# Statistics tiles of nine entries a row instead of five: what moves behind them in SBUF

## The chip, the core and the metric

The kernel runs on one core of a Trainium2 chip. The metric is the device time of one execution in microseconds. A run gives several executions; the median is quoted with the lowest and the highest. A profile is one execution recorded instruction by instruction. TensorE (PE) multiplies, VectorE (DVE) and ScalarE (ACT) do elementwise work, GpSimd (POOL) and SyncE (SP) mostly issue transfers. SBUF is the memory beside the engines: 128 partitions, in each of which a tile takes the same range of bytes.

## The reference

One layer of an encoder on 256 tokens of width 2048, in float32. With `mod = silu(c) @ mod_w + mod_b` cut into six rows of 2048:

```python
hmix = x * (1.0 + sc_m) + sh_m
y = windowed_gqa_sink(hmix, ...)      # q, k, v projection, rotary positions, attention with a sink, output projection
x = layer_norm(alpha * x + (1.0 + g_m) * y, ln_mix_g, ln_mix_b)
hff = x * (1.0 + sc_f) + sh_f
y = square(relu(hff @ w1 + b1)) @ w2 + b2
x = layer_norm(alpha * x + (1.0 + g_f) * y, ln_mlp_g, ln_mlp_b)
```

`layer_norm` takes the mean and the variance of each token's 2048 numbers. The weights are some 290 MB, read once.

## The kernel before, in words

**Numbers.** Every float32 operand is split into a high part that TensorE multiplies in its rounded float32 format (`fp32r`) and a low part that is the rest; a product is three matmuls (high x high, high x low, low x high; `mm3`, lines 556 to 558; in the feed-forward part also lines 1161 to 1163, and 1189 with 1191, where two of the three share one matmul of 512 columns).

**Stages.** The first stage (to about 160 us) computes the modulation vectors and the q, k, v projection; then come attention and its output projection (to about 360 us), the first layer norm, and the feed-forward part in four blocks of 2048 hidden units, the last three of which mix the two weight matrices (`ff_mixed`). The second layer norm and the stores end it.

**The stream of weights.** `Stream` loads the weights in an order written out by hand, 1 MB at a time, into tiles `raw` (line 229, SyncE's queue): 8 KB in each of 128 partitions. Five such buffers last the whole kernel and three more the first stages. From each, ScalarE makes the high part (`wh`, line 299) and VectorE the low part (`wl`, line 250). A raw buffer is loaded again when its readers are done. The modulation weights are either multiplied on TensorE straight from raw (`quad`, line 363) or summed on VectorE (line 403). What shifts the modulated input is `modulated` (lines 579 to 581); line 666 is a filler matmul on a constant tile `onesr`.

**Order.** A scheduler places the instructions by priorities (`first(name)` with the table `AHEAD`), and where `keep_in_program_order` is used, as written. Neither looks at the size of a tile.

**Statistics.** For each token the mean and the variance come from `bn_stats`, six numbers for a piece of a row, and `bn_aggr`, which joins the pieces of a row to mean and variance. The tile `st0` is for tokens 0 to 127, `st1` for 128 to 255. Tokens 0 to 127 have four pieces of 512; tokens 128 to 255 have three of 512 and two of 256, five entries. Both tiles are made twice, for the two layer norms, with two buffers each. The aggregations are at line 864 (in `deviation`) and line 1389.

**Where tiles lie.** Pools are laid out one behind the other in SBUF, each tile rounded up to 32 bytes: constants (`cst`), small tiles (`sml`), then `raws`, `whp`, `wlp`, `gen` and the pool that is first `raws2` and later `gen2`. Inside `sml` the order is that of first use: `sc`, `mrow`, the softmax columns, `warm`, then `st0` and `st1`, then the four temporaries of tag `t2` (rl, uf, sf, tmp, gb, w and others, 2048 bytes each), then the columns of the layer norms. In the kernel before:

| tile | first byte in a partition | over a multiple of 512 |
|---|---|---|
| onesr | 18016 | 96 |
| sc, mrow | 20480, 24576 | 0, 0 |
| st0 (two buffers), st1 (two buffers) | 29312, 29440, 29568, 29696 | 128, 256, 384, 0 |
| temporaries of tag t2 | 29824 and each 2048 on | 128 |
| raw (five buffers) | 38784 and each 8192 on | 384 |
| wh, wl, g, and the late raw and g4b | 79744 and each 4096 on | 384 |

Of the kernel before, what the change touches and what calls it, by code (L numbers as in the profile page):

```python
# [11 lines left out]
F32 = mybir.dt.float32  # L12
# [9 lines left out]
NT = S // 128  # L22
# [39 lines left out]
def hybrid_kernel(ctx: ExitStack, tc: tile.TileContext, a, out: bass.AP):  # L62
    nc = tc.nc
    cst = ctx.enter_context(tc.tile_pool(name="cst", bufs=1))
    sml = ctx.enter_context(tc.tile_pool(name="sml", bufs=4))
# [21 lines left out]
    def g4(dt=F32):  # L87
        return gen.tile([128, 1024], dt, tag="g4", name="g4")
# [102 lines left out]
    def first(name):  # L191
        n = AHEAD.get((stage[0], name), AHEAD.get(name))
        return tc.high_priority(n) if n else nullcontext()
# [358 lines left out]
    def part(tiles, t, c):  # L552
        return tiles[c][:, t * 512:t * 512 + 512]

    def mm3(ps, xh, xl, wh, wl, start, stop):
        nc.tensor.matmul(ps, xh, wh, start=start, stop=False)  # L556
        nc.tensor.matmul(ps, xh, wl, start=False, stop=False)  # L557
        S.prev = nc.tensor.matmul(ps, xl, wh, start=False, stop=stop).ins  # L558
# [277 lines left out]
    def add_gated(ps, t, c, gt, stats, n=1, h=0, counted=True):  # L836
        tmp = sml.tile([128, 512], F32, name="tmp", tag="t2", bufs=4)
        cols = slice(h * 512 // n, (h + 1) * 512 // n)
        z = part(xs, t, c)[:, cols]
        with first("gated"):  # L840
            nc.vector.tensor_tensor(tmp[:, cols], ps[:, cols], gt(c)[:, cols], op=OP.mult)
            nc.vector.tensor_add(z, z, tmp[:, cols])
            if counted:
                nc.vector.bn_stats(stats[t][:, c + h], z)

    def by_halves(ps, factors, gated):

        for h in range(2):
            cols = slice(h * 256, h * 256 + 256)
            for n, (xh, xl, wh, wl) in enumerate(factors):  # L850
                mm3(ps[h][:, cols], xh, xl, wh[:, cols], wl[:, cols], n == 0, n == len(factors) - 1)
            gated(h)

    sc = []
    tight = [False]

    def kept(i):
        return tc.keep_in_program_order(i) if tight[0] else i

    def deviation(st=None, mv=None, between=lambda: None):  # L860
        with first("deviation"):
            if mv is None:
                mv = sml.tile([128, 2], F32, name="mv")
                kept(nc.vector.bn_aggr(mv, st))
            sd = sml.tile([128, 1], F32, name="sd")
            kept(nc.scalar.activation(sd, mv[:, 1:2], AF.Sqrt, bias=eps))
            ve = sml.tile([128, 1], F32, name="ve")
            kept(nc.vector.tensor_scalar_add(ve, mv[:, 1:2], LN_EPS))
            between()
            r0 = sml.tile([128, 1], F32, name="r0")  # L870
            kept(nc.vector.reciprocal(r0, sd))
            q = sml.tile([128, 1], F32, name="qq")
            kept(nc.vector.scalar_tensor_tensor(q, r0, ve, r0, op0=OP.mult, op1=OP.mult))
            kept(nc.vector.scalar_tensor_tensor(q, q, -3.0, r0, op0=OP.add, op1=OP.mult))
        return mv, q

    def normed(c, t):
        mv, rstd = sc[t]
        z = part(xs, t, c)
        with first("normed" if c else "normed0"):  # L880
            if t and c == 1:
                nm = sml.tile([128, 1], F32, name="nmr")
                kept(nc.vector.scalar_tensor_tensor(nm, mv[:, 0:1], -1.0, rstd, op0=OP.mult, op1=OP.mult))
                sc.append(nm)
            if t and c:
                kept(nc.scalar.activation(z, z, AF.Identity, scale=rstd, bias=sc[2]))
            else:
                kept(nc.vector.tensor_scalar(z, z, mv[:, 0:1], rstd, op0=OP.subtract, op1=OP.mult))
# [23 lines left out]
    def project(j, c):  # L912
        wh, wl = S.main()
        oh, ol = oT[j]
        pss = [psa.tile([128, 512], F32, name="pa") for _ in range(NT)]
        last = j == 3 and c == 3
        def of(t, r):
            s = slice(t * 512 + r * 128, t * 512 + r * 128 + 128)
            return oh[:, s], ol[:, s], wh(r), wl(r)

        for t, rs in [(0, range(4))] if last else [(t, (r, r + 1)) for r in (0, 2) for t in range(NT)]:
            for r in rs:
                mm3(pss[t], *of(t, r), r == 0, r == 3)
            if t == 1:
                S.done()
            if t == 1 and rs[0] == 0:
                yield
        if last:
            S.done(False)
            add_gated(pss[0], 0, c, g1, st)  # L930
            sc.append(deviation(st[0][:, :4]))
            normed(0, 0)
            yield
            two = [pss[1], psa.tile([128, 512], F32, name="pa")]
            by_halves(two, [of(1, r) for r in range(4)], lambda h: add_gated(two[h], 1, c, g1, st, 2, h))
            S.done(False)
            turn_over()
            tight[0] = True
            sc.append(deviation(st[1]))
            normed(0, 1)  # L940
            S.nl = NLOW
        with first("project"):
            for t, ps in enumerate(pss):
                if j == 0:
                    nc.vector.tensor_add(part(ys, t, c), ps, bo(c))
                elif j < 3:
                    y = part(ys, t, c)
                    nc.vector.tensor_add(y, y, ps)
                    if j == 2:
                        z = part(xs, t, c)  # L950
                        nc.vector.tensor_mul(y, y, g1(c))
                        nc.vector.scalar_tensor_tensor(z, z, ALPHA, y, op0=OP.mult, op1=OP.add)
                elif not last:
                    add_gated(ps, t, c, g1, st)
# [22 lines left out]
    for n in range(21):  # L977
        j, i = n // 4, n % 4
        if n < 16:
            scores(n)  # L980
        for f in todo:
            f()
        todo = []
        if n == 1:
            S.deep = False
        if n == 5:
            assert all(h is raws for h in S.home[S.at:]), "an early buffer is still in use"
        if n + 1 < len(LATE):
            w = qkv(*LATE[n + 1])
        else:  # L990
            if n == 5:
                ys, bo = [g4b() for _ in range(4)], bias_all(a["bo"], [g4b(), g4b()])
            w = project((n - 5) // 4, (n - 5) % 4)
        mid = mids(n)
        if j < 3:
            if i == 0:
                turn = rope(j + 1, 1)
            if 0 < i < 3 or n and i == 0:
                mid.append(lambda: qA.__setitem__(j + 1, next(turn)))
            if i == 3:  # L1000
                mid.append(lambda: qT.__setitem__(j + 1, pairs_T(qA[j + 1], 4)))
        run(w, mid)
        if n == 0:
            next(turn)
        if 0 < n <= 16 and n % 2 == 0:
            todo.append(values(n - 1))
        if n == 9:

            for c in range(4):
                xs[c] = g4()  # L1010
                i = nc.gpsimd.dma_start(xs[c].rearrange("p (t n) -> p t n", t=NT), a["x"][:, :, 512 * c:512 * c + 512])
                tc.add_manual_dep(i.ins, S.prev.name, AFTER, reason="not sooner")
        if n == 12:
            g1 = gate(m_gm)
        if n == 16:
            warm = sml.tile([128, 1], F32, name="warm")
            nc.scalar.activation(warm, eps, AF.Sqrt)
            st = [sml.tile([128, 5, 6], F32, name=f"st{t}", bufs=2) for t in range(NT)]


    def ff_input(g):
# [299 lines left out]
    for n in range(2):  # L1321
        for h in range(2):
            nc.gpsimd.dma_start(gb[n][h], a["lnrow"][2 + n:3 + n, h * 1024:h * 1024 + 1024].partition_broadcast(128))
    st = [sml.tile([128, 5, 6], F32, name=f"st{t}", bufs=2) for t in range(NT)]
    mid = gather(pm)
    for f in mid[:2]:
        f()
# [26 lines left out]
    mv, rstd = deviation(st[0][:, :4])  # L1354
# [31 lines left out]
    keep = tc.keep_in_program_order  # L1386
    with tc.high_priority(200):
        mv = sml.tile([128, 2], F32, name="mv")
        keep(nc.vector.bn_aggr(mv, st[1]))
        dm = sml.tile([128, 128], F32, name="dm", tag="t2", bufs=4)  # L1390
        keep(nc.vector.tensor_scalar(dm, ident, mv[:, 0:1], 0.5, op0=OP.mult, op1=OP.mult))
        rstd = deviation(mv=mv, between=lambda: keep(nc.vector.scalar_tensor_tensor(
            part(xs, 1, 3), part(xs, 1, 3), mv[:, 0:1], gneg, op0=OP.subtract, op1=OP.mult)))[1]
# [99 lines left out]
```

## Time and profile before

| | |
|---|---|
| median of 3 runs | 1071.91 us (1071.26 to 1072.69) |
| profiled execution | 1070.93 us |
| its span, first to last instruction | 1069.1 us |
| TensorE busy | 1056.9 us (99%) |
| VectorE busy | 941.8 us (88%) |
| ScalarE busy | 619.7 us (58%) |
| mean granted TensorE clock | 0.998 |
| bytes moved by the DMA engines | 292.72 MB, 274 GB/s over the span |

A group in the profile is read as: line, engine, operation, output tile <- input tiles, shapes, count | busy us, mean ns of one | idle time of the engine before them, and what ended it. PE's matmuls overlap, so the mean duration of one is longer than the distance from one to the next. The prediction shows the lines that it uses.

### The profile page before, as it was taken

What the parts mean: (1) busy time and instruction counts of PE and PEld (TensorE: products, weight loads), DVE (VectorE), ACT (ScalarE), POOL (GpSimd) and SP (SyncE); (2) the same over time, 40 slices, a digit from 0 to 9 for tenths busy, and PEclk for the clock granted to TensorE, in tenths of its full rate; (3) what the DMA queues carried; (4) which work ended last, traced back from release to release, by engine and by line L of the source; (5) the groups of instructions that cost most, each with busy time, mean ns of one, the idle gap of its engine ahead of it and who ended that gap; (6) DMA issues with size and microseconds to landing.
All of it is one profiled execution on the core that took longest, in us unless ns stands there. A gap on an engine that the chain in (4) does not pass through costs nothing.

```text
span 1069.1 us, 16015 instructions
## 1 busy us (share of the span) xinstructions
PE 1056.9 (99%) x6181; PEld 858.2 (80%) x6181; DVE 941.8 (88%) x1407; ACT 619.7 (58%) x976; POOL 27.4 (3%) x54
## 2 busy tenths in 40 slices
PE   9999999999999999999999999999999999999998
PEld 7677677666677899988888888888888888888886
DVE  4689999989999898987579899889889987999998
ACT  5433347776772647643367776447677446777740
POOL 1000000001000000000000000000000001000000
PEclk9999999999999999999999999999999999999999
DMA  9999998799965897788624644974564783465642
GB/s 378 419 420 420 418 421 323 274 382 355 385 258 198 335 384 296 273 327 346 243 95 182 236 176 179 354 275 161 193 234 157 292 322 132 163 236 197 256 178 78
DMA packets 43516, 292.72 MB, mean 274 GB/s; under 512 B 5152, under 2 KB 5280, under 8 KB 9648
## 3 DMA queue, kind: packets, MB, share of 16 engines
q1 hardware_dynamic: 39456, 279.85, 67.5%
q0 software_dynamic: 3232, 10.50, 2.9%
q10 hardware_dynamic: 752, 1.35, 0.4%
q8 instruction: 48, 0.79, 0.3%
q14 instruction: 28, 0.23, 0.1%
HBM read 289.57 MB, written 2.11 MB: 273 GB/s over the span
## 4 chain that ended last, share of the span: by engine, by line
PE 91%; DVE 4%; DMA 2%; ACT 2%; issue 1%; DVEq 0%; ACTq 0%
PE pa L556 16%; PE pa L558 15%; PE pa L557 15%; PE pa L1189 15%; PE pa L1191 8%; PE pm L363 4%; PE pa L1163 3%; PE pa L1162 3%; PE pa L1161 3%; PE pa L769 2%; PE pa L830 1%; PE pt L813 1%; PE pa L666 1%; DVE wl L250 1%; DMA raw<-in_w2s 1%; PE pt L557 1%
## 5 line engine op out<-in xcount | busy, mean ns | idle before, releaser
L299 ACT CAST wh<-raw 128x1024 fp32r<-128x1024 f32 (+1 forms) x332 | 336.1, 1020 | 264.8 <-PE pa L558 138.5
L250 DVE TENSOR_TENSOR wl<-raw,wh 128x1024 fp32r<-128x1024 f32 (+1 forms) x332 | 388.5, 1181 | 70.6 <-ACT wh L299 64.4
L556 PE MATMUL pa<-wh,g 128*128 128x512 f32 (+1 forms) x652 | 259.7, 399 | 3.9 <-ACT g L579 3.9
L557 PE MATMUL pa<-wl,g 128*128 128x512 f32 (+1 forms) x652 | 254.7, 391 | 0.0
L558 PE MATMUL pa<-wh,g 128*128 128x512 f32 (+1 forms) x652 | 254.0, 391 | 0.2 <-DVE g L581 0.2
L1189 PE MATMUL pa<-g,wh 128*128 128x512 f32 x768 | 192.4, 392 | 0.1
L1189 PEld LDWEIGHTS pa<-g,wh 128*128 128x128 f32 x768 | 140.5, 188 | 29.6 <-issue 0.8
L556 PEld LDWEIGHTS pa<-wh,g 128*128 128x128 f32 x652 | 122.6, 188 | 41.5 <-issue 6.2
L558 PEld LDWEIGHTS pa<-wh,g 128*128 128x128 f32 x652 | 122.8, 188 | 28.3 <-issue 1.6
L557 PEld LDWEIGHTS pa<-wl,g 128*128 128x128 f32 x652 | 122.9, 188 | 24.6 <-DVE scm L444 0.4
L1191 PEld LDWEIGHTS pa<-g,wl 128*128 128x128 f32 x768 | 104.7, 190 | 7.6
L1191 PE MATMUL pa<-g,wl 128*128 128x256 f32 x768 | 107.0, 282 | 0.0
L403 DVE SCALAR_TENSOR_TENSOR g<-raw,cact,g 128x1024 f32<-128x1024 f32 (+1 forms) x69 | 86.2, 1256 | 1.2 <-DMA raw<-in_modf 0.7
L1161 PE MATMUL pa<-g,wh 128*128 128x256 f32 x240 | 67.9, 285 | 0.4 <-ACT wh L299 0.4
L1163 PE MATMUL pa<-g,wh 128*128 128x256 f32 x240 | 67.6, 285 | 0.0
L1162 PE MATMUL pa<-g,wl 128*128 128x256 f32 x240 | 67.5, 284 | 0.0
L250 DVE TENSOR_TENSOR raw<-raw 128x1024 fp32r<-128x1024 f32 x48 | 58.4, 1221 | 0.7 <-ACT raw L299 0.6
L299 ACT CAST raw<-raw 128x1024 fp32r<-128x1024 f32 x48 | 49.8, 1043 | 5.6 <-DVE raw L261 4.5
L403 DVE SCALAR_TENSOR_TENSOR g4b<-raw,cact,g4b 128x1024 f32<-128x1024 f32 x32 | 40.5, 1277 | 6.9 <-DMA raw<-in_modgf 6.9
L1161 PEld LDWEIGHTS pa<-g,wh 128*128 128x128 f32 x240 | 45.9, 192 | 0.8 <-ACT wh L299 0.8
L1162 PEld LDWEIGHTS pa<-g,wl 128*128 128x128 f32 x240 | 45.8, 192 | 0.7 <-issue 0.4
L599 DVE TENSOR_TENSOR g<-g,pa 128x512 f32<-128x512 f32 x60 | 39.6, 682 | 7.5 <-PE pa L558 7.0
(235 smaller groups left out, 1282.0 us busy)
## 6 DMA issues: line engine op xcount, KB each, us to landing
raw<-in_w1b SPq DMA_DIRECT2D x48, 1024.0 KB, 6.6
raw<-in_w SPq DMA_DIRECT2D x40, 1024.0 KB, 7.3
raw<-in_modm SPq DMA_DIRECT2D x32, 1024.0 KB, 12.0
raw<-in_modf SPq DMA_DIRECT2D x32, 1024.0 KB, 7.0
raw<-in_wqkv SPq DMA_DIRECT2D x24, 1024.0 KB, 14.0
raw<-in_w2s SPq DMA_DIRECT2D x24, 1024.0 KB, 4.9
raw<-in_modgm SPq DMA_DIRECT2D x16, 1024.0 KB, 7.7
raw<-in_wo SPq DMA_DIRECT2D x16, 1024.0 KB, 6.8
```

Of the source, the lines that this page charges most:

```text
L250: self.pinned(nc.vector.tensor_sub(l[:, :w], r, f32(self.hs[n])[:, :w]))
L299: self.pinned(nc.scalar.copy(h[:, :s.shape[-1]], s))
L363: i = nc.tensor.matmul(self.ps[32 * j:32 * j + 32, :w], lhsT[j] if type(lhsT) is list else lhsT, rhs[j], start=self.first, stop=stop)
L403: nc.vector.scalar_tensor_tensor(p[:, :e], s, cact[:, kt:kt + 1], p[:, :e], op0=OP.mult, op1=OP.add)
L556: nc.tensor.matmul(ps, xh, wh, start=start, stop=False)
L557: nc.tensor.matmul(ps, xh, wl, start=False, stop=False)
L558: S.prev = nc.tensor.matmul(ps, xl, wh, start=False, stop=stop).ins
L1161: nc.tensor.matmul(o, wh(w, 128), hh, start=new, stop=False)
L1162: nc.tensor.matmul(o, wl(w, 128), hh, start=False, stop=False)
L1163: nc.tensor.matmul(o, wh(w, 128), hl, start=False, stop=end)
L1189: nc.tensor.matmul(ps, wh(k, 128), ff_in(k), start=k == 0, stop=False)
L1191: nc.tensor.matmul(ps[:, :256], wl(k, 128), ff_in(k)[:, :256], start=False, stop=k == NK - 1)
```

## The change

The statistics tiles have nine entries a row instead of five. What is written to them stays; the two aggregations that read a whole row of `st1` now name its first five entries.

```diff
-            sc.append(deviation(st[1]))
+            sc.append(deviation(st[1][:, :5]))
...
-            st = [sml.tile([128, 5, 6], F32, name=f"st{t}", bufs=2) for t in range(NT)]
+            st = [sml.tile([128, 9, 6], F32, name=f"st{t}", bufs=2) for t in range(NT)]
...
-    st = [sml.tile([128, 5, 6], F32, name=f"st{t}", bufs=2) for t in range(NT)]
+    st = [sml.tile([128, 9, 6], F32, name=f"st{t}", bufs=2) for t in range(NT)]
...
-        keep(nc.vector.bn_aggr(mv, st[1]))
+        keep(nc.vector.bn_aggr(mv, st[1][:, :5]))
```

A buffer of a statistics tile grows from 120 to 216 bytes in a partition, with the rounding from 128 to 224. All tiles behind the four buffers begin 384 bytes later: the large tiles 256 bytes over multiples of 512, the temporaries at multiples of 512.

## The prediction

> **What bounds the kernel now.** I began with the page: busy times, the slices with the granted clock and the transfer rate, and the chain of work that ended last.
>
> ```profile
> span 1069.1 us, 16015 instructions
> PE 1056.9 (99%) x6181; PEld 858.2 (80%) x6181; DVE 941.8 (88%) x1407; ACT 619.7 (58%) x976; POOL 27.4 (3%) x54
> PEclk9999999999999999999999999999999999999999
> DMA  9999998799965897788624644974564783465642
> GB/s 378 419 420 420 418 421 323 274 382 355 385 258 198 335 384 296 273 327 346 243 95 182 236 176 179 354 275 161 193 234 157 292 322 132 163 236 197 256 178 78
> PE 91%; DVE 4%; DMA 2%; ACT 2%; issue 1%; DVEq 0%; ACTq 0%
> ```
>
> TensorE is busy for all but 12.2 us, and nine tenths of the chain is TensorE. The transfers fill the first six slices (about 160 us) at a plateau near 420 GB/s and are loose afterwards. Then I asked for the busy times by stretch.
>
> ```profile
> core 0: us, PE busy (x) PEld busy (x) DVE busy (x) ACT busy (x) POOL busy (x), PEclk, DMA share, GB/s
> 0.00:27.00 27.00, 25.43 (x206) 19.21 (x206) 12.44 (x29) 13.87 (x20) 4.96 (x16) 1.00 0.94 379
> 27.00:160.00 133.00, 127.90 (x970) 93.58 (x967) 115.71 (x168) 50.63 (x67) 1.85 (x2) 0.99 1.01 419
> 160.00:400.00 240.00, 239.27 (x1526) 179.80 (x1525) 225.68 (x425) 153.11 (x340) 9.02 (x14) 1.00 0.83 321
> 400.00:1069.00 669.00, 664.29 (x3488) 565.60 (x3486) 587.97 (x787) 402.05 (x549) 11.62 (x22) 1.00 0.60 224
> ```
>
> TensorE's idle time is 1.6 us at the start, 5.1 us in the saturated stretch, 0.7 us up to 400 us and 4.7 us after that. Whatever the change does to the queues, ScalarE or VectorE can pay only inside these small sums; what it does to each matmul would be paid in full. Two pauses and one slow spell make most of the 5.1 us; I read them in the timelines of TensorE and ScalarE and in the chain (start, us, what; in brackets the idle time before it and its releaser).
>
> ```profile
> 45.51 1.04 ACT L299 CAST wh<-raw 128x1024 fp32r<-128x1024 f32 x1 [2.08 <-PE pa L558]
> 47.11 0.50 PE L556 MATMUL pa<-wh,g 128*128 128x512 f32 x1 [1.64 <-ACT g L579]
> ...
> 114.78 1.99 ACT L299 CAST wh<-raw 128x1024 fp32r<-128x1024 f32 x2 [4.74 <-DMA raw<-in_wqkv]
> 117.33 0.50 PE L556 MATMUL pa<-wh,g 128*128 128x512 f32 x1 [1.23 <-ACT g L579]
> ```
>
> ```profile
> 45.02 0.23 PE pa L557
> ...
> 48.89 0.43 PE pa L557
> ...
> 51.45 0.43 PE pa L557
> ```
>
> The pause before 47.1 us is a loop through TensorE itself: the modulation (L579) stands on ScalarE behind a cast (L299) that waited for a matmul to give back its buffer. After it, matmuls follow each other at 0.43 us instead of 0.23 us until 51.9 us, some seven of them and part of an eighth: about 1.5 us. Only the pause before 117.3 us hangs on a transfer (1.23 us).
>
> **The change part by part.** First, the aggregations. They read the first five entries of each row, the same 30 numbers as before, so no instruction, wait or DMA is added or removed, and no queue is passed.
>
> ```profile
> L864 DVE BATCH_NORM_AGGREGATE mv<-st x3: 254/265/285, 349.4 to 1051.8; 128x2 f32<-128x24 f32 x2, 128x2 f32<-128x30 f32 x1
> L1389 DVE BATCH_NORM_AGGREGATE mv<-st x1: 291/291/291, 1060.9 to 1060.9; 128x2 f32<-128x30 f32 x1
> ```
>
> Two instructions of 30 elements are concerned (one of L864, and L1389). Both lie on the path: the square root on ScalarE waits for them. Six elements more, 24 to 30, cost at most 291 - 254 = 37 ns, so even a form that read a few more would be worth under 0.08 us for both. I take 0.
>
> Second, the addresses. Four statistics buffers (two names, two buffers each) grow from 120 to 216 bytes, that is from 128 to 224 in steps of 32, so everything allocated behind them moves up by 4 x 96 = 384 bytes. Measured against multiples of 512, the large tiles (raw, wh, wl, g, g4b) go from 384 to 256 and the temporaries of tag t2 (rl, uf, sf, tmp, gb, w) from 128 to 0. The tiles ahead of them stay: sc and mrow at 0, onesr at 96. Moved tiles keep their distances from each other, since all shift alike; new are the place against fixed boundaries and the distance to what stayed. The trace has no operation on a tile at 256, so each price comes from the nearest rows: operations of one shape on tiles at 0, 96, 128 and 384.
>
> VectorE and ScalarE (groups by shape, mean ns behind the bar):
>
> ```profile
> L264 DVE TENSOR_TENSOR raw<-raw 128x512 f32<-128x512 f32 x24 | 16.4, 684 | 0.0
> L1123 DVE TENSOR_TENSOR sc<-sf,sc 128x512 fp32r<-128x512 f32 x24 | 16.4, 684 | 0.0
> L581 DVE TENSOR_TENSOR g<-g,g 128x256 fp32r<-128x256 f32 x16 | 6.8, 423 | 0.4
> L1109 DVE TENSOR_TENSOR g<-uf,g 128x256 fp32r<-128x256 f32 x48 | 20.2, 421 | 3.3 <-ACT g L1108 3.3
> L299 ACT CAST wh<-raw 128x512 fp32r<-128x512 f32 x24 | 14.9, 620 | 9.5 <-PE pa L1189 5.8 <-DMA raw<-in_w2s 3.5
> L1122 ACT CAST sc<-sf 128x512 fp32r<-128x512 f32 x24 | 14.8, 617 | 6.1 <-DVE sf L1121 6.1
> ```
>
> With every operand at 384 a subtraction of 512 takes 684 ns; with operands at 128 and 0, also 684. At 256 elements, 423 with all at 384 against 421 with one at 128. The casts take 620 (384 to 384) and 617 (128 to 0). Where two operands share a place, as after the change sf and sc will, the raw-raw row says that sharing is free. I take 0. The bounds are 3 ns an instruction: 1407 + 976 instructions make 7 us of engine time, and at the 4% and 2% of the chain that these engines hold, 3 x 1407 x 0.04 + 3 x 976 x 0.02 is about 0.2 us either way.
>
> TensorE, in the same view and in the timeline (merged runs of one instruction):
>
> ```profile
> L556 PE MATMUL pa<-wh,g 128*128 128x512 f32 x644 | 257.4, 401 | 3.9 <-ACT g L579 3.9
> L1189 PE MATMUL pa<-g,wh 128*128 128x512 f32 x768 | 192.4, 392 | 0.1
> L558 PE MATMUL pa<-wh,sc 128*128 128x512 f32 x24 | 9.8, 408 | 0.0
> L557 PE MATMUL pt<-raw,sc 128*128 128x512 f32 x24 | 9.4, 392 | 0.0
> L557 PE MATMUL pt<-wl,g 128*128 128x512 f32 x24 | 9.5, 396 | 0.0
> L557 PE MATMUL pa<-raw,g 128*128 128x512 f32 x24 | 9.3, 388 | 0.0
> ...
> 12.09 4.59 PE L666 MATMUL pa<-onesr 128*128 128x512 f32 x19
> ...
> 570.50 2.00 PE L1189 MATMUL pa<-g,wh 128*128 128x512 f32 x8
> ```
>
> Nineteen matmuls on onesr, at 96, start (4.59 - 0.40) / 18 = 0.233 us apart; eight on g and wh, at 384, (2.00 - 0.40) / 7 = 0.229 us, the 0.40 being the last one's own duration. A place that is a multiple of 32 only thus costs at most 4 ns more than one that is a multiple of 128. The other comparison is inside the mixed stage of the feed-forward part: its twelve groups of 24 that take their weights from sc (at 0) run from 392 to 408 ns, mean 396; the six groups of 24 that take them from g run from 388 to 396, mean 393. That is 3.4 ns, and it doesn't look like the address: the spread within each set is several times larger, and one tile gives both 392 and 408. I take 0. If the 3.4 ns belong to a distance of 128 between weights and moving rows, they change only for these 288 matmuls: 1.0 us, either way. If they belong to multiples of 256 as such, they would come to every matmul; that is a rival below.
>
> Transfers into raw. All destinations of large loads lie at 384 or 128, so no row shows one at 256 or 0. The nearest rows are the full slices, 418 to 421 GB/s over changing mixtures of loads: 0.7% of 160 us, 1.1 us, is what a slower destination may cost by them. A gain of any size reaches the end only through the 1.23 us before 117.3 us, since the larger pause is fed by TensorE. Bounds: -1.2 to +1.1 us. I take 0, the middle: the plateau looks like one rate that the loads share.
>
> [...]
>
> The sum: 0 + 0 + 0 + 0 on the profiled execution's 1070.9 us (span 1069.1, and 1.8 us around it), which is 1.0 us under the median of the runs. So I forecast the median again: **1071.9 us**.
>
> **The rivals.** (1) The loads get shorter. The wait before 117.3 us closes, 1.2 us: 1070.7 us. If the earlier arrivals also take away the pause that comes before the slow spell, its 1.5 us go as well: 1071.9 - 2.7 = 1069.2 us. For it: the share of 1.01 over 133 us. Against it: TensorE's larger pause is fed by TensorE, and behind 160 us the queues have slack (0.83, 0.60), so an earlier load only waits longer.
>
> (2) Slower: a matmul whose rows lie at multiples of 256 costs 3.4 ns more, as the groups on sc hint. The place is every 128x512 matmul: 3 x 644 of L556 to L558, 768 of L1189, and eighteen groups of 24, together 3132. The price is 3132 x 3.4 ns = 10.6 us: 1082.5 us. It decides from 2.1 us / 3132 = 0.7 ns each. Against it: 0.233 and 0.229 us at 96 and at 384, and weight reads that belong to one tile and yet differ by 16 ns.
>
> (3) The mirror of it: TensorE's fixed cost per matmul falls at 256. One nanosecond each is 3.1 us: 1068.8 us. Nothing in the rows is for it, since finer alignment from 96 to 384 bought at most 4 ns, and that between idle fillers and real work.
>
> (4) The change doesn't do what it says: the order of instructions shifts with the tile sizes, or the tiles land elsewhere. Tags, buffer counts and priorities are untouched, so I expect the same order; if it shifted, the saturated stretch could win or lose a pause such as the one before 47.1 us with its slow spell, 1.6 + 1.5 = 3.1 us: 1068.8 or 1075.0 us.
>
> **How the numbers follow.** About 0.2%, or 2.1 us, is what a measurement of this kernel can tell from no change. Chances: no effect 0.64; rival (1) 0.15, of which rather more than half, 0.09, ends below 1069.8; (2) 0.10; (3) 0.06; (4) 0.05, 0.02 faster, 0.02 slower and 0.01 within. So faster 0.09 + 0.06 + 0.02 = 0.17; slower 0.10 + 0.02 and 0.01 for the 1 us on sc together with the scatter of the runs = 0.13; the same 0.70. The range runs from 1068.8, the lower ends of (1) and (3), to 1074.2, 2.1 us of indistinguishable time plus 0.2 us of VectorE and ScalarE above the forecast (a slower destination's 1.1 us lies inside); most of (2) and the upper half of (4) stay outside.
>
> **What would show it.** After the change, the subtraction of 512 should still take 684 ns, the casts 617 to 620, the matmul runs 0.23 us apart, the aggregation of 30 elements about 291 ns, and the plateau of the first slices should stay at 418 to 421 GB/s. A plateau clearly higher would be rival (1), and then the wait of 4.74 us for in_wqkv should shrink; runs of eight matmuls longer or shorter than 2.00 us would be (2) or (3); another count of instructions or another order of lines would be (4). The forecast is wrong if any group of the same shape moves by more than its few nanoseconds, or if TensorE's 12.2 us of idle time change by more than 2 us.

## The result, and the profile after

The changed kernel takes 1067.58 us in the median (1066.59 to 1069.32) against 1071.91 us (1071.26 to 1072.69): a ratio of 0.9962, 95% interval 0.9949 to 0.9976. It is 4.3 us faster, where no change was forecast, and lies below the lower end of the forecast range, 1068.8 us. The order of the instructions on every engine is the same as before.

The page of the profile after, and the first two stretches:

```profile
span 1065.4 us, 16015 instructions
PE 1054.3 (99%) x6181; PEld 858.3 (81%) x6181; DVE 941.3 (88%) x1407; ACT 619.7 (58%) x976; POOL 27.4 (3%) x54
GB/s 380 426 424 426 415 426 313 281 378 356 392 253 198 334 377 302 271 337 339 251 85 193 236 172 178 357 282 149 207 228 168 283 320 138 167 237 199 253 181 79
```

```profile
0.00:27.00 27.00, 25.43 (x207) 19.31 (x208) 12.30 (x29) 13.94 (x21) 4.96 (x16) 1.00 0.94 381
27.00:160.00 133.00, 128.88 (x971) 94.36 (x971) 116.72 (x169) 50.71 (x68) 1.85 (x2) 0.99 1.01 423
```

TensorE is busy 2.6 us less for the same work and idle 1.1 us less (11.1 instead of 12.2 us). Four of the five full slices stand at 424 to 426 GB/s where they stood at 418 to 421, and the saturated stretch as a whole at 423 instead of 419. VectorE and ScalarE are as they were; two groups of the profile after, and the aggregation of line 1389:

```profile
L1123 DVE TENSOR_TENSOR sc<-sf,sc 128x512 fp32r<-128x512 f32 x24 | 16.4, 685 | 0.0
L1122 ACT CAST sc<-sf 128x512 fp32r<-128x512 f32 x24 | 14.8, 617 | 5.6 <-DVE sf L1121 5.6
...
L1389 DVE BATCH_NORM_AGGREGATE mv<-st x1: 291/291/291, 1057.2 to 1057.2; 128x2 f32<-128x30 f32 x1
```

Where the time went: first, the wait for a load in the first stage. The timelines after (TensorE and ScalarE):

```profile
46.91 0.50 PE L556 MATMUL pa<-wh,g 128*128 128x512 f32 x1 [1.64 <-ACT g L579]
...
113.52 1.99 ACT L299 CAST wh<-raw 128x1024 fp32r<-128x1024 f32 x2 [3.73 <-DMA raw<-in_wqkv]
116.07 0.49 PE L556 MATMUL pa<-wh,g 128*128 128x512 f32 x1 [0.22 <-ACT g L579]
```

The load that ended at 114.8 us ends at 113.5, and TensorE's pause behind it shrinks from 1.23 to 0.22 us. The pause before 47 us, fed by TensorE itself, is 1.64 us as before.

Second, the mixed stage of the feed-forward part. The chain in time (start, us, what), its runs of L1189 over one cycle and the first run of the next, before and after:

```profile
576.95 1.86 PE pa L1189 x8
579.76 1.84 PE pa L1189 x8
583.93 1.83 PE pa L1189 x8
586.72 1.84 PE pa L1189 x8
...
593.01 1.86 PE pa L1189 x8
```

```profile
575.62 1.81 PE pa L1189 x8
578.39 1.84 PE pa L1189 x8
582.57 1.81 PE pa L1189 x8
585.33 1.84 PE pa L1189 x8
...
591.55 1.81 PE pa L1189 x8
```

A cycle takes 593.01 - 576.95 = 16.06 us before and 591.55 - 575.62 = 15.93 us after. The runs of eight that follow matmuls on sc (1.86, 1.83) become 1.81; those that don't follow such matmuls stay at 1.84. The matmuls on sc themselves (nanoseconds: shortest/median/longest), before and then after:

```profile
L556 PE MATMUL pa<-wh,sc x24: 390/404/404, 558.5 to 1015.3; 128*128 128x512 f32 x24
...
L557 PE MATMUL pm<-raw,sc x24: 390/404/404, 560.3 to 1016.9; 128*128 128x512 f32 x24
```

```profile
L556 PE MATMUL pa<-wh,sc x24: 389/389/396, 557.2 to 1011.6; 128*128 128x512 f32 x24
...
L557 PE MATMUL pm<-raw,sc x24: 389/389/397, 559.1 to 1013.3; 128*128 128x512 f32 x24
```

Two rows measure both effects in every kernel: the first start of L769 (the first scores of attention, so the end of the first stage) and the first and last start of L1189 (the mixed stage, whose length is taken as the time between the two). Before, then after:

```profile
L769 PE MATMUL pa<-g,g x128: 376/376/480, 164.8 to 309.8; 64*128 64x256 f32 x128
...
L1189 PE MATMUL pa<-g,wh x768: 387/389/499, 540.3 to 1005.4; 128*128 128x512 f32 x192
```

```profile
L769 PE MATMUL pa<-g,g x128: 376/376/480, 163.7 to 308.6; 64*128 64x256 f32 x128
...
L1189 PE MATMUL pa<-g,wh x768: 389/389/499, 539.1 to 1001.8; 128*128 128x512 f32 x192
```

The first stage ends 1.1 us sooner and the mixed stage takes 462.7 instead of 465.1 us: 3.5 of the 3.7 us between the spans.

### The profile page after: what moved, and what is told of

The parts are those of the page before. It is cut to its first block, busy times and chain, and to the rows that moved or that the text cites. A ratio compares the mean times of both kernels' runs of the same rounds, so it can differ in the third digit from the quotient of the medians.

```text
span 1065.4 us, 16015 instructions
## 1 busy us (share of the span) xinstructions
PE 1054.3 (99%) x6181; PEld 858.3 (81%) x6181; DVE 941.3 (88%) x1407; ACT 619.7 (58%) x976; POOL 27.4 (3%) x54
## 4 chain that ended last, share of the span: by engine, by line
PE 94%; DVE 2%; ACT 1%; DMA 1%; issue 0%; DVEq 0%; ACTq 0%
PE pa L1189 16%; PE pa L556 16%; PE pa L558 15%; PE pa L557 15%; PE pa L1191 9%; PE pm L363 4%; PE pa L1163 3%; PE pa L1162 3%; PE pa L1161 3%; PE pa L769 2%; PE pa L830 1%; PE pt L813 1%; PE pa L666 1%; PE pt L557 1%; PE pt L556 1%; PE pt L558 1%
## 5 line engine op out<-in xcount | busy, mean ns | idle before, releaser
L558 PE MATMUL pa<-wh,g 128*128 128x512 f32 (+1 forms) x652 | 253.9, 391 | 0.2 <-DVE g L581 0.2
L1189 PE MATMUL pa<-g,wh 128*128 128x512 f32 x768 | 191.3, 391 | 0.0
L1189 PEld LDWEIGHTS pa<-g,wh 128*128 128x128 f32 x768 | 140.7, 188 | 27.9 <-issue 0.8
L558 PEld LDWEIGHTS pa<-wh,g 128*128 128x128 f32 x652 | 122.7, 188 | 28.5 <-issue 1.6
L1191 PEld LDWEIGHTS pa<-g,wl 128*128 128x128 f32 x768 | 104.8, 190 | 7.5
L1191 PE MATMUL pa<-g,wl 128*128 128x256 f32 x768 | 107.1, 282 | 0.0
```

Source lines behind the costliest of these rows:

```text
L1189: nc.tensor.matmul(ps, wh(k, 128), ff_in(k), start=k == 0, stop=False)
L1191: nc.tensor.matmul(ps[:, :256], wl(k, 128), ff_in(k)[:, :256], start=False, stop=k == NK - 1)
```

## The experiments

Two theories stood after the result. **Destination**: a load into a raw buffer that begins on a multiple of 256 bytes is faster than one into a buffer that doesn't. **Distance**: a matmul is slower where the place of its weights and the place of the rows that stream past them, both over multiples of 256, differ. Rivals: the place of the streamed rows alone; the temporaries; the nine entries themselves. In all experiments the order of the instructions is that of the kernel before and nothing is left out of the computation; only unused bytes move tiles.

**Only the large tiles moved** (384 to 256; statistics tiles of five entries).

```diff
-                nm = sml.tile([128, 1], F32, name="nmr")
+                nm = sml.tile([128, 32], F32, name="nmr")[:, :1]
```

> Statistics tiles as before; a column tile behind the temporaries is made larger instead, so that the large tiles (raw, wh, wl, g, g4b) go from 384 to 256 over multiples of 512 and the temporaries stay at 128. If the large tiles alone carry the gain (transfers and TensorE), all of it is here: about 4 us faster than before (ratio 0.996), the wait for in_wqkv before 114.8 us falls from 4.74 to about 3.7 us, and the eight L1189 matmuls behind the groups on sc take 1.81 us instead of 1.86 or 1.83. If the temporaries matter (VectorE and ScalarE), part of the 4 us is missing.

Measured: 1066.73 us, ratio 0.9957 (0.9943 to 0.9970), the whole gain. Its lines L769 and L1189, and its saturated stretch:

```profile
L769 PE MATMUL pa<-g,g x128: 376/376/480, 163.3 to 308.2; 64*128 64x256 f32 x128
...
L1189 PE MATMUL pa<-g,wh x768: 387/389/499, 538.3 to 1001.1; 128*128 128x512 f32 x192
```

```profile
27.00:160.00 133.00, 127.17 (x972) 93.38 (x972) 116.61 (x169) 50.89 (x67) 1.91 (x2) 1.00 1.01 425
```

The load again ends 1.4 us sooner, at 113.37 us, and the runs on L1189 are 1.81 us. The idle time of ScalarE in front of that load, which I had named as a mark, is a bad one: it was 5.47 us here, longer than before, because ScalarE had finished its earlier work sooner. The end of the first stage is the better mark. The clock column reads 1.00: this execution had no slow spell at 48 us, and still the first stage ended only 0.4 us before that of the kernel after, which had one. Most of what the clock gives there is taken back at the later load: TensorE's pause behind it is 1.96 us here and 0.22 us in the kernel after.

**Only the temporaries moved** (128 to 0; nine entries, large tiles back at 384).

```diff
-    st = [sml.tile([128, 5, 6], F32, name=f"st{t}", bufs=2) for t in range(NT)]
+    st = [sml.tile([128, 9, 6], F32, name=f"st{t}", bufs=2) for t in range(NT)]
...
-                nm = sml.tile([128, 1], F32, name="nmr")
+                nm = sml.tile([128, 16], F32, name="nmr")[:, :1]
```

> Statistics tiles of nine entries, and the column tile behind the temporaries larger, so that the temporaries go from 128 to 0 and the large tiles come back to 384. If the large tiles carry the gain: no change, ratio 1.000, wait for in_wqkv 4.7 us, L1189 runs of 1.86 and 1.83 us. If the nine entries or the temporaries carry it: about 4 us faster, ratio 0.996.

Measured: 1071.96 us, ratio 1.0002 (0.9994 to 1.0011).

```profile
L769 PE MATMUL pa<-g,g x128: 376/376/480, 166.0 to 311.0; 64*128 64x256 f32 x128
...
L1189 PE MATMUL pa<-g,wh x768: 387/389/499, 541.4 to 1006.2; 128*128 128x512 f32 x192
```

```profile
27.00:160.00 133.00, 125.92 (x960) 91.51 (x959) 114.29 (x167) 49.27 (x65) 1.90 (x2) 0.99 1.01 420
```

Neither the nine entries nor the place of the temporaries changes the time by more than the interval's 0.1%. The mixed stage takes 464.8 us, as slow as before.

**sc moved to the place of the large tiles** (sc and mrow from 0 to 384, mrow's second buffer to 448, the rest as before).

```diff
-    b2 = cst.tile([128, NK], F32, name="b2")
+    b2 = cst.tile([128, NK + 96], F32, name="b2")
...
-            self.r = sml.tile([128, 512], F32, name="mrow", bufs=2)
+            self.r = sml.tile([128, 528], F32, name="mrow", bufs=2)[:, :512]
```

> Large tiles and temporaries as before (384 and 128), but sc and mrow moved from 0 to 384, so that the weights in sc lie at the same place over a multiple of 512 as the rows that stream past them. If the slow matmuls of the mixed stage come from the distance of 128 between sc and the large tiles: L1189 runs of 1.81 us and 2.0 us gained in the mixed stage, while the wait for in_wqkv stays at 4.7 us and the rate at 419 GB/s; ratio about 0.998. If the place of the large tiles as such sets the matmuls' speed: no change, ratio 1.000.

Measured: 1069.93 us, ratio 0.9982 (0.9973 to 0.9991).

```profile
L769 PE MATMUL pa<-g,g x128: 376/376/480, 166.2 to 311.2; 64*128 64x256 f32 x128
...
L1189 PE MATMUL pa<-g,wh x768: 389/389/499, 541.8 to 1004.5; 128*128 128x512 f32 x192
```

```profile
27.00:160.00 133.00, 126.02 (x960) 92.03 (x959) 114.28 (x167) 49.25 (x65) 1.91 (x2) 0.99 1.01 420
```

The mixed stage is as short as after the change (462.7 us) with every large tile still at 384, while the first stage keeps its late end and its 420 GB/s. So the place of the streamed rows by itself isn't what counts for TensorE.

**Only the five lasting raw buffers moved** (384 to 256; wh, wl, g, g4b and the three early raw buffers stay at 384).

```diff
-                nm = sml.tile([128, 1], F32, name="nmr")
+                nm = sml.tile([128, 32], F32, name="nmr")[:, :1]
...
     raws = ctx.enter_context(tc.tile_pool(name="raws", bufs=RAWS))
+    gap = ctx.enter_context(tc.tile_pool(name="gap", bufs=1))
...
+    room = gap.tile([128, 32], F32, name="room")
```

> Only the five lasting raw buffers go from 384 to 256 (the three early ones and all of wh, wl, g, g4b stay at 384, sc at 0, temporaries at 128). If the destination of the loads sets their speed: rate in the saturated stretch between 419 and 423 GB/s, nearer to 423, wait for in_wqkv down by 0.6 to 1.0 us, ratio about 0.999. In the mixed stage the distance theory expects the matmuls that stream raw past sc to speed up and those that stream wh and wl past sc to stay slow: 0.5 to 1.5 us of the 2.0. If the loads' speed comes from anything else than the destination, the rate stays 419 GB/s and the wait 4.7 us.

Measured: 1068.69 us, ratio 0.9978 (0.9969 to 0.9988).

```profile
L769 PE MATMUL pa<-g,g x128: 376/376/480, 163.4 to 308.5; 64*128 64x256 f32 x128
...
L1189 PE MATMUL pa<-g,wh x768: 387/389/499, 538.7 to 1003.2; 128*128 128x512 f32 x192
```

```profile
27.00:160.00 133.00, 126.73 (x969) 92.98 (x969) 116.49 (x169) 50.56 (x67) 1.93 (x2) 1.00 1.01 425
```

The place of the five lasting raw buffers alone brings the whole gain of the first stage, more than expected (I had set the ratio at 0.999). But it isn't each load's own destination that does it. The three early buffers lie at 384 here (203136, 211328 and 219520), as in the second experiment, at the very same addresses. Between 27 and 160 us a packet (one row of 8192 bytes) of the 18 loads into them takes 309.3 ns in the mean, as little as one of the 34 loads into the buffers at 256 (310.3); in the second experiment it takes 314.0. So the loads into buffers at 384 were fast here, where most loads around them go to 256. The destination theory as stated is refuted; whether the fast loads come from the other loads' destinations or from the engines' reads of the five buffers, no run here separates.

The mixed stage stays slow, 464.5 us; I had expected 0.5 to 1.5 us there from the matmuls that stream raw past sc. I had overlooked that raw at 256 now stands apart from the weights in g at 384. Two runs of L1189 in the chain of this kernel show it:

```profile
575.33 1.82 PE pa L1189 x8
...
582.29 1.86 PE pa L1189 x8
```

The first follows matmuls of raw on sc, which now lie together: 1.82 us instead of 1.86. The second follows matmuls of raw on g, which now lie apart: 1.86 instead of 1.83. What one pair gained the other lost, as the distance theory has it.

**Large tiles at 0**, sc at 0, temporaries at 128: the edit of the first experiment with 16 in place of 32.

> Large tiles at 0 over multiples of 512 (256 in the kernel after), sc at 0, temporaries at 128. If multiples of 256 are what counts, for the destination of the loads and for the distance between weights and streamed rows: the same as e1_large_only, ratio 0.995 to 0.997, rate 425 GB/s in the saturated stretch, L1189 runs of 1.81 and 1.84 us. If multiples of 512 count, more is gained than there: ratio below 0.994. If a distance of exactly 256 between sc and the large tiles was what helped the matmuls: runs of 1.86 us again and 2 us of the gain missing.

Measured: 1067.28 us, ratio 0.9955 (0.9942 to 0.9967).

```profile
L769 PE MATMUL pa<-g,g x128: 376/376/480, 163.6 to 308.4; 64*128 64x256 f32 x128
...
L1189 PE MATMUL pa<-g,wh x768: 387/389/501, 538.4 to 1001.4; 128*128 128x512 f32 x192
```

The same as at 256 in both stages (mixed: 463.0 us): the multiple of 512 brought no more than 256 did (1066.73 us).

**Large tiles at 256, sc 128 apart from them** (sc and mrow at 128).

```diff
-    b2 = cst.tile([128, NK], F32, name="b2")
+    b2 = cst.tile([128, NK + 32], F32, name="b2")
...
-                nm = sml.tile([128, 1], F32, name="nmr")
+                nm = sml.tile([128, 24], F32, name="nmr")[:, :1]
```

> Large tiles at 256 as after the change, but sc and mrow at 128, so that weights in sc and streamed rows lie 128 apart again (temporaries at 256). Distance theory: the mixed stage is as slow as before (L1189 runs of 1.86 and 1.83 us, 1.9 us lost against e1_large_only), while the loads keep their gain: rate near 425 GB/s, ratio about 0.9975. If the place of the large tiles, or of sc, against a boundary counted and not their distance: either nothing lost (ratio 0.996), as the rows stay at 256, or a new price for weights at 128 that shows in the L1189 runs with other numbers than 1.86 and 1.83.

Measured: 1069.18 us, ratio 0.9978 (0.9967 to 0.9988).

```profile
L769 PE MATMUL pa<-g,g x128: 376/376/480, 163.7 to 308.7; 64*128 64x256 f32 x128
...
L1189 PE MATMUL pa<-g,wh x768: 387/389/499, 538.9 to 1003.7; 128*128 128x512 f32 x192
```

The converse of the third experiment: the first stage is fast and the mixed one slow again (464.8 us), with the same 1.86 and 1.83 us in the chain as before the change. With it, the distance theory holds for sc in both directions and at different absolute places.

**The constants moved too**: large tiles, sc, mrow, ident and onesr all at 256.

```diff
-    pack = cst.tile([128, 242], F32, name="pack")
+    pack = cst.tile([128, 282], F32, name="pack")[:, :242]
...
-    b2 = cst.tile([128, NK], F32, name="b2")
+    b2 = cst.tile([128, NK + 24], F32, name="b2")
...
-                nm = sml.tile([128, 1], F32, name="nmr")
+                nm = sml.tile([128, 16], F32, name="nmr")[:, :1]
```

> All that TensorE reads at 256 over multiples of 512: the large tiles, sc, mrow, and also the constants ident and onesr (96 in the other kernels). If the distance counts for all matmuls, the transposes through ident in attention (L747, L813, L1039) get faster as well: some 200 of them, up to 10 ns each, 2 us on top of e1_large_only, ratio about 0.994. If it counts only where a run of full-width matmuls is interrupted, as with sc: ratio 0.996, no more than e1_large_only.

Measured: 1066.96 us, ratio 0.9956 (0.9944 to 0.9969).

```profile
L769 PE MATMUL pa<-g,g x128: 376/376/480, 163.2 to 308.2; 64*128 64x256 f32 x128
...
L1189 PE MATMUL pa<-g,wh x768: 387/389/499, 538.3 to 1001.4; 128*128 128x512 f32 x192
```

No more than the first experiment: the transposes through ident (128 columns) don't feel it; those of L747 take 272 to 273 ns in the median in either kernel. The three best versions, with ratios of 0.9955 to 0.9957, can't be told from the changed kernel: they lie inside its interval.

**Large tiles at 288**, 32 off: the first experiment and a gap of 32 bytes in front of the raw buffers (a tile of [128, 8] in a pool of its own).

> Large tiles at 288, 32 bytes off the 256 of e1_large_only; sc at 0, temporaries at 128. If only the remainder of 256 counts for the loads, they are as slow as at 384 (419 GB/s) or slower, and the wait for in_wqkv comes back; if a small offset is milder, the rate lies between 419 and 425. For the matmuls: if any distance that isn't a multiple of 256 slows them, runs of 1.86 us or longer; if it is the distance of 128 that collides, 1.81 us stay. Ratio from 0.996 (neither) to 1.000 or above (both).

Measured: 1070.85 us, ratio 0.9988 (0.9977 to 0.9999).

```profile
L769 PE MATMUL pa<-g,g x128: 376/376/480, 165.1 to 310.2; 64*128 64x256 f32 x128
...
L1189 PE MATMUL pa<-g,wh x768: 387/389/499, 540.1 to 1003.8; 128*128 128x512 f32 x192
```

```profile
27.00:160.00 133.00, 127.37 (x964) 93.22 (x965) 115.34 (x168) 50.44 (x67) 1.85 (x2) 0.99 1.01 418
```

For the loads, 32 off is as bad as 128 off (418 GB/s, first stage to 165.1 us, against 419 and 164.8 before). For the matmuls it is milder: the runs behind them stay at 1.81 us and the mixed stage takes 463.7 us, 0.8 of the 1.9 us that a distance of 128 costs.

Put together, the ten profiles fall into groups without overlap. The slow spell of the clock has to be looked at with them: in the profiles before and after, the granted clock is 0.5 for 3.4 us. It is not always behind the pause at 47 us: in the second and third experiment it comes behind the pause at 117 us, and three profiles have none. Four microseconds in the second experiment and in the first (the clock is the third number from the end):

```profile
117.00:121.00 4.00, 3.73 (x21) 1.84 (x22) 3.86 (x10) 1.69 (x4) 0.00 (x0) 0.57 1.01 422
```

```profile
117.00:121.00 4.00, 4.00 (x23) 2.84 (x16) 3.86 (x9) 0.62 (x2) 0.00 (x0) 1.00 1.01 428
```

| | kernels | first stage ends at, us | mixed stage, us |
|---|---|---|---|
| lasting raw at a multiple of 256, no slow spell | three | 163.2 to 163.4 | |
| the same, spell at 48 us | after and two others | 163.6 to 163.7 | |
| raw 128 or 32 off, spell at 48 us | before and one other | 164.8 and 165.1 | |
| raw 128 off, spell at 117 or 119 us | two | 166.0 and 166.2 | |
| sc and large tiles apart by a multiple of 256 | after and four others | | 462.7 to 463.1 |
| apart by 32 more | one | | 463.7 |
| apart by 128 more (in the fourth experiment wh and wl from sc, and raw from g) | before and three others | | 464.5 to 465.1 |

The mixed stages differ by 464.8 - 462.9 = 1.9 us in the mean. The first stages differ by 165.5 - 163.5 = 2.0 us, but that mixes two things. With the spell at 48 us in both, the place of raw is worth 1.3 us. Without it there, it is worth 2.8 us: at 384 the spell then comes behind the later pause, and at 256 it doesn't come at all; the 1.5 us more fit an estimate of 1.7 us for the spell, half of its 3.4 us. The runs say the same of the spell: a mean clock of 0.999 or 1.000, which leaves no room for one, is on record for 18 of 40 executions with the lasting raw buffers at a multiple of 256, and for 1 of 79 with raw elsewhere. Why the spell follows a pause in one execution and not in another stays open: in the third and the fourth experiment the pause at 117 us is equally long, 2.41 and 2.40 us, and only the third has a spell behind it.

The two means add up to 3.9 us, and the medians of the runs differ by 4.3. By times alone, 0.9978 for raw and 0.9982 for sc give 0.9960 together, and 0.9957 was measured with both.

## Why the prediction was wrong

**What held.** The aggregations cost nothing (line 1389 takes 291 ns before and after), VectorE and ScalarE took as long at the new addresses (L1123: 684 and 685 ns, L1122: 617 and 617), the order of the instructions didn't move, and rivals (2), (3) and (4) didn't occur. The place of a matmul's rows by itself has no price: 384, 256 and 0 give the same mixed stage when sc lies at the same remainder of 256 (462.7, 462.7 and 463.0 us).

**The step on TensorE failed.** I had the right row in hand: groups on sc slower than groups on g by 3.4 ns. I put it to 0 with the words that the spread within each set is larger and one tile gives both 392 and 408. Most of that spread was the effect: with sc at the right distance the medians of the two groups above fall from 404 to 389 ns, and the third and sixth experiments switch it off and on by moving sc. (The 408 itself, L558 on wh and sc, was not part of it. It is 409 after the change; a few matmuls of some 500 ns make this mean.)

The bound that I kept, 1.0 us for 288 matmuls, nearly held for the matmuls on sc alone: from start to start, the 264 of them within the mixed stage take 62.2 us before and 61.1 after. It left out the matmuls behind them: the 768 of L1189, whose own weights and rows keep their distance, take 176.6 us before and 175.5 after. So the term was 1.9 us instead of 0, outside its bound. The starts show how the delay runs on. Settled matmuls start 227 ns apart, in either kernel. Behind a run of L1191, the next five on g start 233, 236, 228, 233 and 231 ns apart before they settle, also after the change. Before the change such a settling begins anew where matmuls on sc meet others: the eight of L1189 behind raw on sc start 235, 233, 236, 224, 231, 236, 228 and 233 ns apart, where after the change all are at 227. And in the fourth experiment the matmuls of raw on sc, together now but among others that are apart, take 46.2 us in the stage, against 46.3 before and 45.6 after. So it seems to be the change of distance from one matmul to the next that costs, and not a distance held; that reading is argued from the starts, no run tests it alone.

**The step on the transfers failed in what it left out.** I took the common plateau of 418 to 421 GB/s for one rate that the loads share. All destinations stood 128 off; with the lasting buffers on multiples of 256 it is 422 to 425 in the saturated stretch. And I let the gain reach the end only through the 1.23 us pause. That pause did close by 1.0 us, and with the spell at 48 us in both kernels the gain of the first stage is 1.3 us, about my bound of 1.2. What the bound had no room for is the slow spell: my profile showed one, behind a pause that no load feeds, and I reckoned with no execution in which it stands elsewhere or is missing. TensorE's waits at line 556 (us in total, times, longest), before and in the second experiment:

```profile
PE pa L556 <- ACT g L579: 3.9, 4, 1.6
```

```profile
PE pa L556 <- ACT g L579: 5.2, 4, 2.5
```

In the second experiment the clock is full at 48 us, the pause at 117 us is twice as long, and the spell follows it. Of the three profiles with raw at 384, the one that I worked from has the shortest first stage. Over the profiles at hand the term was 2.0 us, against a bound of 1.2.

Rival (1) with its 1.2 to 2.7 us was right for the first stage at both ends, 1.3 and 2.8 us; only the spell that goes is the one at 117 us, and it goes in part of the executions. It knew nothing of the mixed stage. I had no rival that held both halves, and the chance of 0.17 for faster was too low.

Over the saturated stretch the rate rose by 0.7 to 1.4%, from 419 GB/s to between 422 and 425. A packet of 8192 bytes takes 314.4 ns in the mean before and 310.4 after, 1.3% less, and 33% against 99% of them take 310 ns or less. At 288 a packet takes 315.6 ns, no less than at 384, and in the fourth experiment loads to 384 take 309.3 ns. What shortens the packets, no run here shows.

## What to carry to other kernels

Try it with the load buffers at multiples of 256 bytes, and with all tiles that TensorE uses together as weights and as streamed rows at the same remainder of 256; a few unused bytes in a small tile ahead of them do it, and here that was worth 4.3 of 1071.9 us. Where groups of equal matmuls differ and the difference repeats from cycle to cycle, as medians of 404 and 392 ns did here among the groups on sc before the change, look at where their operands lie before calling it noise. And judge a saturated stretch by several profiles, and by where the slow spells of the clock lie in each: here the same place of raw was worth 1.3 or 2.8 us in the first stage, depending on them.

## What the runs showed of the hardware

- Loads of 1 MB (8 KB in each of 128 partitions) into SBUF moved at 422 to 425 GB/s in the saturated stretch when the five lasting buffers began on multiples of 256 bytes, and at 418 to 420 when all buffers were 32 or 128 off. A load's own destination didn't decide it: among loads to multiples of 256, loads to 384 take 309.3 ns a packet, and among loads to 384 the same addresses take 314.0. The mechanism stays open.
- A run of 128x512 matmuls was delayed where weights came from a tile whose remainder of 256 differs by 128 from that of the streamed rows, amid matmuls where it doesn't: medians of 404 instead of 389 ns in two of the groups, and up to 0.05 us more in the next eight matmuls (1.86 against 1.81 us). A difference of 32 cost 0.8 us over the stage where one of 128 cost 1.9. The time went with the place of the one relative to the other: the stage takes 462.7 us with sc and the large tiles both at 384, and 464.8 us with sc at 128 and the large tiles at 256. What inside the memory or the engine makes it so stays open.
- Transposes of 128 columns against a constant tile showed no such effect: those of L747 take 272 to 273 ns in the median with the tile 160 off and with it at the same remainder.
- The executions differed in the clock: a spell of 3.4 us at a granted clock of 0.5 came behind a pause of 1.64 us, or behind a later one of 2.4 to 2.5 us, or not at all.
